# Two of the four A softmax tiles turned by VectorE and transfers instead of TensorE, in a two-layer encoder trunk

## The chip, the cores and the metric

The kernel runs on one core of one Trainium2 chip. The metric is the time of one execution in device microseconds, as the median of several runs; lower is better. TensorE (PE in the profile) multiplies and also turns 128x128 blocks, VectorE (DVE) and ScalarE (ACT) do elementwise work, GpSimd (POOL) a few small things, and SyncE (SP) issues most of the transfers (DMAs). Each engine works through a queue of its own in order.

## The reference

The model is an encoder of two layers over 256 tokens of width 1024, all in float32. Cut to what matters here:

```python
for l in range(2):
    x = x + 0.5 * swiglu(rms_norm(x, ffn1_norm[l]), ...)       # width 2816
    h = rms_norm(x, mix_norm[l])
    qa, ka, va, qb, kb, vb = jnp.split(h @ w_in[l], SPLITS, axis=-1)
    out_a = windowed_gqa_sink(qa, ka, va, sink[l], slopes_a)   # A: 8 query heads, 2 key/value heads, width 64
    out_b = differential_attention(qb, kb, vb, lam, slopes_b)  # B: 4 heads, two softmaxes each, values of width 128
    out_b = rms_norm(out_b, diff_subln[l]) * (1 - lam_init)
    x = x + jnp.concatenate([out_a, out_b], -1) @ w_out[l]
    x = x + 0.5 * swiglu(rms_norm(x, ffn2_norm[l]), ...)
return rms_norm(x, final_norm)
```

In group A a token sees the tokens within 128 of it, with a linear distance penalty, and the sum under the softmax has one more term, the head's learned sink. In group B the second softmax, times lambda, is subtracted from the first.

## The kernel before

All weights come from device memory as float32 and are split on the chip into a high part (ScalarE casts it, `act.copy`) and a low part (VectorE subtracts, `emit_split`); a product is then three matmuls (high x high, low x high, high x low). A weight tile of 1 MB is a `Step`; `specs` lists all steps in the order of use. `weights()` takes the next step and calls `ahead()`, which writes out the transfers up to ten steps ahead (six raw tiles, `N_RAW`) and the splits six half tiles ahead (seven pairs of split tiles, `N_W`). The transfers are issued on SP at line 186 and wait there until a split has freed a raw tile.

`mix(l, norm, nxt_norm)` is the attention of one layer. Its order of work:

1. Projections with the tokens on the free axis: B keys, B queries, A keys and values (`tkv`), A queries (two steps of 256 columns, `qA0`, `qA1`). `q_finish` and `k_finish` scale and split them.
2. `scores` does the products of two heads: four groups of three matmuls for each head and half, in two banks of PSUM. VectorE adds the distance penalty and takes the minimum in one instruction (`tensor_tensor_reduce`, CUSTOM_DVE in the profile); ScalarE takes the exponential with its sum. `soft_b` combines the two softmaxes of a B head on VectorE. `soft_a` handles one pair of A heads (c and c + 4): it adds the sink, takes the reciprocal, and then VectorE multiplies the four 128x256 parts by it (lines 962 to 966). Tokens are on the partitions.
3. The products with the values need the keys on the partitions. `keys_first` turns a 128x1024 tile: TensorE transposes eight 128x128 blocks into two banks, ScalarE copies one bank out and VectorE the other. It is called twice for B (`aT`) and four times for A (`pT`), so 48 transposes in each layer.
4. The B values (`vB`): two steps of four 128-row blocks (`k0` = 0 and 4), 24 matmuls each; then ScalarE scales the two halves out of PSUM. Both halves hold keys, so every B output needs both.
5. `values_a(0)` and `values_a(1)` multiply the A values with `pT`, two head pairs each, and split the results into `oT[0]` and `oT[1]`; then the B products into `osl`, `norm_b` (squares on ScalarE, sum on VectorE, power on GpSimd, product on VectorE), and `operands_b`, which turns them on TensorE into `oT[2]` and `oT[3]`.
6. The output projection: four steps of `w_out`; step k0 uses `oT[k0 // 2]`. The steps come in the order 0, 2, 4, 6, and `operands_b` stands in the middle of the second.

While `kept[0]` is true, each instruction is pinned behind the one written before it for its engine. It is set to False from the first keys to the end of part 4: there the framework's scheduler orders each engine's queue when the program is built, by readiness in its own model of time and, among ready instructions, by their place in the text. `urgent()` moves what stands in it 300 places forward in that preference. From `values_a(0)` on the written order holds.

`Blocks` is the other way of turning, in use for hidden values and norms: `take` transposes 32x32 blocks of a 128x512 half on VectorE (STREAM_TRANSPOSE), `move` issues four transfers of 128 KB from SBUF to SBUF (line 350) which carry the blocks to their partitions, and `turned` gives a view of the result. It takes two buffers of the pool `s4`, from which most tiles of the attention come as well (14 buffers).

Of the kernel before, what the change touches and what calls it, by code (L numbers as in the profile page):

```python
# [14 lines left out]
P = 128  # L15
D = 1024
# [48 lines left out]
def trunk(ctx: ExitStack, tc: tile.TileContext, x, n1, g1, u1, d1, nm, w_in, sink,  # L65
# [49 lines left out]
    def urgent():  # L115

        return tc.high_priority(300)
# [159 lines left out]
    for l in range(DEPTH):  # L277
# [52 lines left out]

# [534 lines left out]
    def ffn_close(parts, nxt, flips):  # L865
# [22 lines left out]
        res.squares(0)  # L888
        nxt.late = res.late

    def mix(l, norm, nxt_norm):
        kbs = {}
        den_b = tmp("den_b", 1, (P, HB, 4))
# [58 lines left out]
        def soft_a(c, q):  # L952
            ns = nsnk[:, l, c].rearrange("p t s -> p (t s)")
            den = den_a[:, c]
            e, negm = scores(q, kbs["a"], distA, [slopeA[c], slopeA[c + 4]], [ns[:, n:n + 1] for n in range(4)], den)
            es = tmp("es", 4, (P, 4))
            dve.tensor_tensor(es, negm, snk[:, l, c].rearrange("p t s -> p (t s)"), op=ALU.add)
            act.activation(es, es, AF.Exp)
            r = tmp("ra", 4, (P, 4))
            dve.tensor_tensor(r, den, es, op=ALU.add)  # L960
            dve.reciprocal(r, r)
            for t in range(2):
                for a in range(2):
# [8 lines left out]
        k_finish(rmul(s1), 2, [("b", 2), ("b", 3)])  # L972
        q0 = q_finish(ngroup(norm, weights()), [qscB[:, 0:1], qscB[:, 1:2]])
        q1 = q_finish(ngroup(norm, weights()), [qscB[:, 2:3], qscB[:, 3:4]])
        a_b = [soft_b(0, q0[0]), soft_b(1, q0[1])]


# [7 lines left out]
        for kc in range(2):  # L985
            pe.transpose(vsl[:, kc, 0:P], tkv[:, 1, kc * P:(kc + 1) * P], ident)
        act.copy(vA, vsl[:, :, 0:P])
        qA1 = q_finish(ngroup(norm, weights()), [qscA[:, 2:3], qscA[:, 3:4]])
        p_a = [soft_a(0, qA0[0]), soft_a(1, qA0[1])]

        def keys_first(pick):

            out_ = blk(F32)
            for kc in range(2):
                tsl = bank()
                for i in range(4):
                    pe.transpose(tsl[:, i * P:(i + 1) * P], pick(kc, i), ident)
                (act.copy if kc == 0 else dve.tensor_copy)(out_[:, kc], tsl)
            return out_

        def keys_first_b(hp):
            return keys_first(lambda kc, i: a_b[2 * hp + i // 2][:, i % 2, kc * P:(kc + 1) * P])

        def keys_first_a(c):
            return keys_first(lambda kc, i: p_a[c][:, i % 2, (i // 2) * 256 + kc * P:(i // 2) * 256 + (kc + 1) * P])

        aT = [keys_first_b(0)]
        vB = tp.tile([P, 2, 512], F32, tag="v", bufs=1, name=nm_("v"))
        vsl = [bank() for _ in range(2)]
        for k0 in (0, 4):  # L1010
            w = weights()
            for k in range(4):
                kk = k0 + k
                hi, lo = w.part(k)
                xv = norm.xs[kk // 2][:, kk % 2]
                for t in range(2):
                    xh, xl = xv[:, t * P:(t + 1) * P], xv[:, S + t * P:S + (t + 1) * P]
                    pe.matmul(vsl[t], lhsT=xh, rhs=hi, start=kk == 0, stop=False)
                    pe.matmul(vsl[t], lhsT=xl, rhs=hi, start=False, stop=False)
                    pe.matmul(vsl[t], lhsT=xh, rhs=lo, start=False, stop=kk == KC - 1)  # L1020
# [48 lines left out]
        def values_a(cp):  # L1069

            o = [bank() for _ in range(2)]
            for i in range(2):
                for kc in range(2):
                    for a in range(2):
                        j, f0 = (i + a) % 2, slice(a * 64, a * 64 + 64)
                        pe.matmul(o[j][f0, 0:S], lhsT=vA[:, kc, f0], rhs=pT[2 * cp + j][:, kc, a * 256:a * 256 + 256],
                                  start=kc == 0, stop=kc == 1)
# [13 lines left out]
        on = norm_b()  # L1091
        accs = [[bank(), bank()] for _ in range(2)]
        res = Residual(nxt_norm, accs)
# [13 lines left out]
        w = weights()  # L1107
        out_part(w, 6, 0, BY_TOKENS)
        for c in range(2):
# [115 lines left out]
```

## Time and profile before

| | |
|---|---|
| median of 3 runs | 909.76 us (909.72 to 910.09) |
| the profiled execution, its own time | 909.62 us |
| its span in the profile | 907.8 us |
| TensorE busy | 898.3 us (99%) |
| VectorE busy | 730.1 us (80%) |
| ScalarE busy | 559.7 us (62%) |
| transfers | 209.25 MB, mean 231 GB/s |

The span is what the profiler records from the first instruction to the last; 1.8 us of the execution's time lie outside of it. A row of the timeline gives the start in us, the time to the end of the last of the instructions merged in it, the engine, the line, the operation, what is written and read, the shape and the count; in brackets stands how long the engine was idle before and what released it. Almost all instructions bear line 80, a helper, so they are told apart by tiles: `s` is a buffer of the pool `s4`, `w` a split weight tile, `v` the B values, `ps` a bank of PSUM. The end of a matmul is modelled, so the pace on TensorE is taken from the starts.

### The profile page before, as it was taken

The page shows a single profiled execution, that of the slowest core. Times are in us where ns is not written, and L with a number is a line of the kernel's source. Part 1 is how long each engine was busy: PE and PEld are TensorE (multiplying, and loading weights), DVE is VectorE, ACT ScalarE, POOL GpSimd, SP SyncE. Part 2 cuts the span into 40 slices and gives each one's busy share as a digit, 9 for nine tenths or more (in the row PEclk, how much of TensorE's full clock was granted, in tenths as well). Part 3 has the DMA queues.
Part 4 walks back from the last instruction along what each step waited for, and adds up shares of the span by engine and source line. Part 5 has one row for each costly group of instructions (what it writes and reads, how often), then busy time and mean ns, then how long its engine had stood idle before and what let it go on. Part 6 is the DMA issues. An engine that isn't in the chain of part 4 may idle for free.

```text
span 907.8 us, 12665 instructions
## 1 busy us (share of the span) xinstructions
PE 898.3 (99%) x4546; PEld 756.2 (83%) x4546; DVE 730.1 (80%) x1106; ACT 559.7 (62%) x913; POOL 52.4 (6%) x72
## 2 busy tenths in 40 slices
PE   9999999999999999999999999999999999999997
PEld 7888888899888888888888888888997888888886
DVE  6689998879965789988768988887798667988883
ACT  7766665567744776665565755665676465755661
POOL 0401000000000001000000000000000000000001
PEclk9999999999999999999999999999999999999999
DMA  9989999856424879999759799997643459799921
GB/s 343 320 250 321 328 246 320 223 154 190 136 81 151 249 199 318 328 247 311 234 159 288 187 343 291 298 278 210 185 142 95 139 133 271 192 339 313 296 69 46
DMA packets 131262, 209.25 MB, mean 231 GB/s; under 512 B 5502, under 2 KB 51648, under 8 KB 131200
## 3 DMA queue, kind: packets, MB, share of 16 engines
q1 hardware_dynamic: 115808, 181.17, 60.0%
q0 software_dynamic: 12928, 25.46, 16.1%
q10 hardware_dynamic: 2464, 1.84, 0.8%
q8 instruction: 35, 0.57, 0.3%
q14 instruction: 27, 0.22, 0.1%
HBM read 192.71 MB, written 1.05 MB: 213 GB/s over the span
## 4 chain that ended last, share of the span: by engine, by line
PE 88%; DVE 5%; ACT 3%; DMA 2%; issue 2%; SPq 0%; POOLq 0%; POOL 0%; DVEq 0%; ACTq 0%
PE ps L80 88%; DVE w L80 2%; DVE s L80 2%; DMA raw<-in_ffn_w_gate_dram 1%; ACT s L80 1%; ACT w L80 1%; DMA raw<-in_ffn_w_up_dram 1%; DVE tmp L80 0%; ACT junk L80 0%; ACT tmp L80 0%; DVE ra L80 0%; ACT L80 0%; SPq L189 0%; DVE xk L80 0%; POOLq L1220 0%
## 5 line engine op out<-in xcount | busy, mean ns | idle before, releaser
L80 PE MATMUL ps<-w,s 128*128 128x512 f32 (+1 forms) x2994 | 683.2, 389 | 0.4 <-DVE s L80 0.4
L80 PEld LDWEIGHTS ps<-w,s 128*128 128x128 f32 x2994 | 558.4, 188 | 115.5 <-DVE s L80 0.7
L80 DVE TENSOR_TENSOR w<-raw,w 128x1024 fp32r<-128x1024 f32 (+1 forms) x416 | 435.1, 1087 | 97.1 <-ACT w L80 90.6
L80 ACT CAST w<-raw 128x1024 fp32r<-128x1024 f32 (+1 forms) x416 | 375.7, 942 | 172.6 <-PE ps L80 126.5
L80 PE MATMUL ps<-s,w 128*128 128x256 f32 x672 | 84.0, 285 | 0.0
L80 PEld LDWEIGHTS ps<-s,w 128*128 128x128 f32 x672 | 81.7, 191 | 1.1
L80 PE MATMUL ps<-w,q 128*128 128x512 f32 x288 | 69.4, 390 | 0.0
L80 PEld LDWEIGHTS ps<-w,q 128*128 128x128 f32 x288 | 54.0, 188 | 11.6 <-issue 0.4
L80 DVE STREAM_TRANSPOSE s<-s 128x512 f32<-128x512 f32 (+1 forms) x48 | 46.1, 999 | 0.0
L80 POOL DMA_DIRECT2D raw<-in_ffn_w_up_dram x16 | 21.0, 1314 | 400.8 <-DVE ms L80 150.1
L80 ACT CAST s<-s 128x256 fp32r<-128x256 f32 x88 | 29.3, 402 | 17.2 <-DMA s<-s 17.2
L80 ACT ACTIVATE s<-s,negm 128x256 f32<-128x256 f32 x64 | 31.9, 500 | 8.7 <-DVE negm L80 8.7
L80 DVE TENSOR_TENSOR s<-s,s 128x256 fp32r<-128x256 f32 x88 | 31.6, 421 | 5.5 <-ACT s L80 5.5
L80 ACT ACTIVATE tmp<-ps,r 128x512 f32<-128x512 f32 (+1 forms) x40 | 24.9, 644 | 13.3 <-PE ps L80 12.7
L80 ACT CAST q<-tmp 128x512 fp32r<-128x512 f32 x20 | 12.3, 616 | 31.3 <-DVE tmp L80 31.3
L80 ACT ACTIVATE junk<-xk 128x512 f32<-128x512 f32 x24 | 15.1, 631 | 19.0 <-issue 18.5
L80 PE MATMUL ps<-w,v 128*128 128x512 f32 x96 | 23.4, 391 | 0.2 <-DVE w L80 0.2
L80 ACT ACTIVATE s<-s,gcol 128x256 fp32r<-128x256 f32 (+1 forms) x40 | 17.0, 502 | 8.4 <-DMA s<-s 8.4
L80 ACT ACTIVATE tmp<-tmp,r 128x512 f32<-128x512 f32 x8 | 5.8, 725 | 26.2 <-DVE tmp L80 26.2
L80 PEld LDWEIGHTS ps<-w,v 128*128 128x128 f32 x96 | 17.9, 188 | 4.3 <-DVE w L80 0.6
L80 DVE TENSOR_TENSOR q<-tmp,q 128x512 fp32r<-128x512 f32 x20 | 14.1, 703 | 8.3 <-ACT q L80 8.3
L80 DVE SCALAR_TENSOR_TENSOR s<-ps,hr,tmp 128x512 f32<-128x512 f32 (+1 forms) x32 | 20.4, 678 | 0.0
(117 smaller groups left out, 430.7 us busy)
## 6 DMA issues: line engine op xcount, KB each, us to landing
raw<-in_ffn_w_down_dram SPq DMA_DIRECT2D x44, 1024.0 KB, 8.5
raw<-in_ffn_w_gate_dram SPq DMA_DIRECT2D x39, 1024.0 KB, 5.9
raw<-in_ffn_w_up_dram SPq DMA_DIRECT2D x39, 1024.0 KB, 7.2
raw<-in_ffn_w_up_dram POOLq DMA_DIRECT2D x16, 1024.0 KB, 10.3
raw<-in_w_in_dram SPq DMA_DIRECT2D x14, 1024.0 KB, 5.8
s<-s SPq DMA_DIRECT2D x98, 128.0 KB, 4.6
raw<-in_ffn_w_gate_dram POOLq DMA_DIRECT2D x8, 1024.0 KB, 9.8
raw<-in_ffn_w_gate_dram SPq DMA_DIRECT2D x8, 512.0 KB, 5.6
```

What stands on the lines that cost most here:

```text
L80: ins = issue(*a, **k)
```

## The change

Two of the four A softmax tiles (c = 0 and 1) go through `Blocks` instead of `keys_first`; the last multiplication of `soft_a` goes from VectorE to ScalarE for all four; and the order around them changes. `keys_first_b(0)` moves in front of the last A query projection, the second step of the B values does one half of the tokens after the other (`BY_VALUES`), `keys_first_b(1)` moves behind the B values and is `urgent`, as are the splits in `values_a`. `values_a(0)` stands between the two halves of the B products, the other two A tiles are turned on TensorE behind them, `values_a(1)` moves behind `operands_b`, and the `w_out` steps come in the order 0, 4, 2, 6 in `specs` and in use.

```diff
-        for k0 in (0, 2):
+        for k0 in (0, 4, 2, 6):
...
-            specs.append(Step(2, D, o_moves))
-        for k0 in (4, 6):
-            specs.append(plain(wo, 0, D, k0, 2))
+            specs.append(Step(2, D, o_moves) if k0 < 4 else plain(wo, 0, D, k0, 2))
...
+    BY_VALUES = {0: [(t, k) for k in range(4) for t in range(2)], 4: [(t, k) for t in range(2) for k in range(4)]}
...
-                    dve.tensor_scalar_mul(w_, w_, r[:, 2 * t + a:2 * t + a + 1])
+                    act.mul(w_, w_, r[:, 2 * t + a:2 * t + a + 1])
...
+        def keys_turned(c):
+
+            turn = Blocks(by_block=False)
+            for t in range(2):
+                turn.take(p_a[c][:, t], t)
+            turn.move()
+            return turn.turned().rearrange("p (a k) y j -> p a k y j", a=2)
...
         aT = [keys_first_b(0)]
+        qA1 = q_finish(ngroup(norm, weights()), [qscA[:, 2:3], qscA[:, 3:4]])
+        p_a = [soft_a(0, qA0[0]), soft_a(1, qA0[1])]
+
+        pT = [keys_turned(c) for c in range(2)]
...
-            for k in range(4):
+            for t, k in BY_VALUES[k0]:
...
             if k0 == 0:
                 p_a += [soft_a(2, qA1[0]), soft_a(3, qA1[1])]
-                aT.append(keys_first_b(1))
-                pT = [keys_first_a(0)]
...
-        for c in range(1, 4):
-            pT.append(keys_first_a(c))
...
-            for j in range(2):
-                split(oT[cp][:, j:j + 1], o[j][:, 0:S].unsqueeze(1))
+            with urgent():
+                for j in range(2):
+                    split(oT[cp][:, j:j + 1], o[j][:, 0:S].unsqueeze(1))
 
         kept[0] = True
-        values_a(0)
-        values_a(1)
+        with urgent():
+            aT.append(keys_first_b(1))
         osl = [bank() for _ in range(2)]
...
+            if t == 0:
+                values_a(0)
+        pT += [keys_first_a(c) for c in (2, 3)]
         on = norm_b()
...
-        for k0 in (0, 2):
+        w = weights()
+        for h in range(2):
+            out_part(w, 0, h)
+        operands_b(on)
+        values_a(1)
+        for k0 in (4, 2):
             w = weights()
             for h in range(2):
                 out_part(w, k0, h)
-                if (k0, h) == (2, 0):
-                    operands_b(on)
-        w = weights()
-        for h in range(2):
-            out_part(w, 4, h)
         w = weights()
         out_part(w, 6, 0, BY_TOKENS)
```

More of the change, by code (lines that the diff above doesn't have):

```diff
@@ L974, in mix, with keys_first, keys_first_a, keys_first_b @@
         q1 = q_finish(ngroup(norm, weights()), [qscB[:, 2:3], qscB[:, 3:4]])
+        def keys_first(pick):
+            out_ = blk(F32)
+            for kc in range(2):
+                tsl = bank()
+                for i in range(4):
+                    pe.transpose(tsl[:, i * P:(i + 1) * P], pick(kc, i), ident)
+                (act.copy if kc == 0 else dve.tensor_copy)(out_[:, kc], tsl)
+            return out_
+        def keys_first_a(c):
+            t_ = keys_first(lambda kc, i: p_a[c][:, i % 2, (i // 2) * 256 + kc * P:(i // 2) * 256 + (kc + 1) * P])
+            return t_.rearrange("p k (a y j) -> p a k y j", a=2, j=32).rearrange("p a k y j -> p a k y j")
+        def keys_first_b(hp):
+            return keys_first(lambda kc, i: a_b[2 * hp + i // 2][:, i % 2, kc * P:(kc + 1) * P])
+        def keys_turned(c):
[4 more added lines that the diff above has]
+            return turn.turned().rearrange("p (a k) y j -> p a k y j", a=2)
         a_b = [soft_b(0, q0[0]), soft_b(1, q0[1])]
@@ L987, in mix @@
         act.copy(vA, vsl[:, :, 0:P])
+        aT = [keys_first_b(0)]
         qA1 = q_finish(ngroup(norm, weights()), [qscA[:, 2:3], qscA[:, 3:4]])
         p_a = [soft_a(0, qA0[0]), soft_a(1, qA0[1])]
[L991 to L1007, printed above, removed]
+        pT = [keys_turned(c) for c in range(2)]
         vB = tp.tile([P, 2, 512], F32, tag="v", bufs=1, name=nm_("v"))
@@ L1015, in mix @@
                 xv = norm.xs[kk // 2][:, kk % 2]
[L1016 to L1020, printed above, removed]
+                xh, xl = xv[:, t * P:(t + 1) * P], xv[:, S + t * P:S + (t + 1) * P]
+                pe.matmul(vsl[t], lhsT=xh, rhs=hi, start=kk == 0, stop=False)
+                pe.matmul(vsl[t], lhsT=xl, rhs=hi, start=False, stop=False)
+                pe.matmul(vsl[t], lhsT=xh, rhs=lo, start=False, stop=kk == KC - 1)
             if k0 == 0:
                 p_a += [soft_a(2, qA1[0]), soft_a(3, qA1[1])]
-                aT.append(keys_first_b(1))
-                pT = [keys_first_a(0)]
         act.activation(vB[:, 0], vsl[0], AF.Copy, scale=norm.r[:, 0:1])
         act.activation(vB[:, 1], vsl[1], AF.Copy, scale=norm.r[:, 1:2])
-        for c in range(1, 4):
-            pT.append(keys_first_a(c))
         oT = [blk() for _ in range(4)]
@@ L1075, in values_a @@
                         j, f0 = (i + a) % 2, slice(a * 64, a * 64 + 64)
-                        pe.matmul(o[j][f0, 0:S], lhsT=vA[:, kc, f0], rhs=pT[2 * cp + j][:, kc, a * 256:a * 256 + 256],
+                        pe.matmul(o[j][f0, 0:S], lhsT=vA[:, kc, f0], rhs=pT[2 * cp + j][:, a, kc],
                                   start=kc == 0, stop=kc == 1)
-            for j in range(2):
-                split(oT[cp][:, j:j + 1], o[j][:, 0:S].unsqueeze(1))
+            with urgent():
+                for j in range(2):
+                    split(oT[cp][:, j:j + 1], o[j][:, 0:S].unsqueeze(1))
         kept[0] = True
-        values_a(0)
-        values_a(1)
+        with urgent():
+            aT.append(keys_first_b(1))
         osl = [bank() for _ in range(2)]
```

## The prediction

> **What bounds the kernel now.** I read the page's shares first, then who TensorE waited for, then TensorE's own order of work in the attention of layer 0. The page and the view of the waits:
>
> ```profile
> PE 898.3 (99%) x4546; PEld 756.2 (83%) x4546; DVE 730.1 (80%) x1106; ACT 559.7 (62%) x913; POOL 52.4 (6%) x72
> ...
> PE 88%; DVE 5%; ACT 3%; DMA 2%; issue 2%; SPq 0%; POOLq 0%; POOL 0%; DVEq 0%; ACTq 0%
> ```
>
> ```profile
> PE ps L80 <- DVE s L80: 1.6, 3, 0.6
> PE ps L80 <- DVE tmp L80: 1.4, 1, 1.4
> PE ps L80 <- DVE w L80: 0.2, 1, 0.2
> ```
>
> TensorE sets the time: it is busy almost throughout and waits 3.2 us in all. Only two things shorten this kernel, less work on TensorE and fewer of its few waits; and every new wait of TensorE is paid in full. The timeline of TensorE in the stretch that the change touches (start, us, count):
>
> ```profile
> 229.14 1.69 PE L80 MATMUL ps<-s,q 64*128 64x256 f32 x24
> 230.76 1.09 PE L80 MATMUL ps<-ident,s 128*128 128x128 f32 x8
> 231.61 5.74 PE L80 MATMUL ps<-w,s 128*128 128x512 f32 x24
> 237.28 1.69 PE L80 MATMUL ps<-s,q 64*128 64x256 f32 x24
> 238.90 1.09 PE L80 MATMUL ps<-ident,s 128*128 128x128 f32 x8
> 239.74 4.84 PE L80 MATMUL ps<-w,s 128*128 128x512 f32 x20
> 244.42 1.04 PE L80 MATMUL ps<-ident,s 128*128 128x128 f32 x8
> 245.21 1.17 PE L80 MATMUL ps<-w,s 128*128 128x512 f32 x4
> 246.22 1.03 PE L80 MATMUL ps<-ident,s 128*128 128x128 f32 x8
> 247.88 2.45 PE L80 MATMUL ps<-ident,s 128*128 128x128 f32 x16 [0.62 <-DVE s L80]
> 250.26 3.67 PE L80 MATMUL ps<-s,vA 128*64 128x256 f32 x32
> 253.86 3.84 PE L80 MATMUL ps<-v,s 128*128 128x128 f32 x32
> 257.45 8.44 PE L80 MATMUL ps<-w,s 128*128 128x512 f32 x36
> 265.74 1.03 PE L80 MATMUL ps<-ident,s 128*128 128x128 f32 x8
> ```
>
> Eight transposes take 0.85 (230.76 to 231.61), 0.84 and 0.79 us: 0.10 each. From 244.42 to 250.26, 5.84 us, stand 32 transposes of the four A tiles and four matmuls (1.01 us). At 0.10 the 32 would take 3.2; so 1.63 us of waiting lie in this stretch, some of it marked (0.62 for the multiplied weights), some inside the merged rows. Layer 1 shows the same (693.95, again 0.62), so I work out one layer and double it.
>
> ```profile
> 693.95 2.45 PE L80 MATMUL ps<-ident,s 128*128 128x128 f32 x16 [0.62 <-DVE s L80]
> ```
>
> **The change, part by part.** TensorE loses the transposes of c = 0 and 1: 16 x 0.10 = 1.6 us. The other 16 move behind work that doesn't need them, so the 1.63 us of waiting can go too: at most 3.2 us a layer. Where TensorE would then stand, with no new wait, is a sum of starts. The A queries end 0.85 later, since the first B tile is turned in front of them: 229.99. Scores 1.62, B values 5.67, scores 1.62, B values 5.69, the second B tile 0.84: the B products start at 245.43. Half of them (3.59 / 2 = 1.80) to 247.23, `values_a(0)` (3.60 / 2 = 1.80) to 249.03, the other half to 250.83, 16 transposes to 252.43; there `w_out` 0 starts. Before it starts at 257.45, but with `values_a(1)` behind it, so the break-even is 257.45 - 1.80 = 255.65.
>
> Now what must be ready at these times. ScalarE gets the 16 multiplications. Rows of it, by group on the page and from the timelines:
>
> ```profile
> L80 ACT ACTIVATE s<-s,negm 128x256 f32<-128x256 f32 x64 | 31.9, 500 | 8.7 <-DVE negm L80 8.7
> ```
>
> ```profile
> 231.76 0.51 ACT L80 ACTIVATE s<-s,negm 128x256 f32<-128x256 f32 x1 [0.93 <-DVE negm L80]
> ...
> 237.44 1.12 ACT L80 CAST w<-raw 128x512 fp32r<-128x512 f32 x2
> ...
> 237.96 2.19 DVE L80 TENSOR_SCALAR s<-s,ra 128x256 f32<-128x256 f32 x8
> ...
> 246.80 0.28 ACT L80 ACTIVATE es<-es 128x4 f32<-128x4 f32 x2
> 246.99 0.56 ACT L80 COPY s<-ps 128x512 f32<-128x512 f32 x1
> ...
> 247.46 1.25 ACT L80 ACTIVATE v<-ps,r 128x512 f32<-128x512 f32 x2
> ...
> 252.33 0.65 ACT L80 CAST s<-ps 128x256 fp32r<-128x256 f32 x2 [1.44 <-PE ps L80]
> ```
>
> ```profile
> 290.82 1.71 ACT L80 ACTIVATE s<-s,gcol 128x256 fp32r<-128x256 f32 x4 [0.64 <-DMA s<-s]
> ```
>
> VectorE did a multiplication in 2.19 / 8 = 0.27. A 128x256 part by a per-partition factor on ScalarE is the row at 290.82: 1.71 / 4 = 0.43, so 6.8 us for 16. The Trainium skill, ScalarE: Activation LUTs, section Rules for kernel authors, gives multiplications to VectorE and not to ScalarE, which speaks against this part; the rows agree, 0.43 against 0.27. By the rule, with the 16 left on VectorE, ScalarE's sum below would be 14.4 us in place of 21.2, and VectorE's 4.4 more.
>
> Is ScalarE free for it? From the first exponential of the A heads (231.76 before, 0.85 later after: 232.6) it has, until the last weights are multiplied: 16 exponentials at 0.50 = 8.0, three pairs of weight casts at 1.12 = 3.4, two rows of sinks at 0.28 = 0.6, the multiplications 6.8, the B values out of PSUM 1.25, a copy for the second B tile 0.56, the split of `values_a(0)` 0.65: 21.2 us. That ends at 253.8 if it is never idle. The eight transposes of c = 3 need the last of it, where TensorE alone would be there at 251.6. So ScalarE is the **new bound** of this stretch: `w_out` 0 starts at 253.8 + 0.8 = 254.6, not at 252.43. Against 255.65 that gains 1.05 us. If the last pair of casts falls behind the multiplications, as nothing needs it soon, it is 2.2; if ScalarE idles 1.1 us for data, nothing. I take 1.2 us a layer, the middle.
>
> VectorE loses 16 x 0.27 = 4.4 us and two copies, and gets four block transposes:
>
> ```profile
> 308.82 2.04 DVE L80 STREAM_TRANSPOSE s<-s 128x512 f32<-128x512 f32 x2
> 310.78 2.32 DVE L80 TENSOR_TENSOR w<-raw,w 128x1024 fp32r<-128x1024 f32 x2
> 310.92 2.50 SPq L350 DMA_DIRECT2D s<-s  x4
> ```
>
> ```profile
> 158.02 2.52 SPq L350 DMA_DIRECT2D s<-s  x4
> ...
> 163.01 0.71 ACT L80 CAST s<-s 128x256 fp32r<-128x256 f32 x2 [0.35 <-DMA s<-s]
> ```
>
> Two transposes take 2.04, so 4.1 us; VectorE is relieved. Four transfers take SP 2.5 us to issue, and from the first issue to the use 5.0 us pass (158.02 to 163.01, with a wait for the transfer at the end). The multiplications of c = 0, 1 began at 237.96 before. One after the other from 238.0 on ScalarE, c = 0 is done at 239.7, c = 1 at 241.4; their block transposes end at about 240.8 and 242.8. SP issues c = 0 to 243.3, then c = 1; it lands 5.0 after 243.3, at 248.3. `values_a(0)` wants it at 247.2: 1.1 us late, but the wait for ScalarE comes earlier or covers it, so I don't add it.
>
> SP carries eight more issues, 5 us, and its weight loads stand behind them:
>
> ```profile
> SPq L186 <- DVE ra L80: 16.9, 2, 8.5
> ```
>
> ```profile
> 237.67 0.37 SPq L186 DMA_DIRECT2D raw<-in_ffn_w_up_dram  x1
> 246.57 28.23 SPq L186 DMA_DIRECT2D raw<-in_ffn_w_gate_dram  x4
> ```
>
> The load at 237.67 had waited 8.5 us for its raw tile, without any wait of TensorE for weights; I cost loads that come 5 us later at nothing, and at up to 1 us a layer if the splits run late.
>
> `norm_b` must be done when `w_out` 0 ends. Before:
>
> ```profile
> 257.74 0.60 ACT L80 ACTIVATE tmp<-ps 128x512 f32<-128x512 f32 x1 [1.19 <-PE ps L80]
> ...
> 261.09 1.29 DVE L80 TENSOR_TENSOR s<-ps,rb 128x512 f32<-128x512 f32 x2 [1.75 <-POOL rb L80]
> ```
>
> From the end of the B products (257.45) to the scaled result (262.38) pass 4.93 us; after, 16 transposes and 24 matmuls (7.3 us) cover it, less the two copies in front of the squares on ScalarE (about 2 us). It holds by some tenths. Between `operands_b` and `w_out` 4 stands `values_a(1)`, 1.8 us, beside the 12 matmuls that covered it before (2.8); I cost that at 0 to 0.5. The order of the `w_out` loads moves no bytes. Matmuls that read `pT` in runs of 32 are shown nowhere; nothing below, and 1.8 us a layer above if `values_a(0)` took twice its time; as the nearest row, the plain `values_a`, is not limited by reading, I take nothing.
>
> The sum: 2 x 1.2 = 2.4 us less. The profiled execution took 909.62 with a span of 907.8; from the median of 909.76 it gives **907.4 us**. Its own range is 2 x 0 to 2 x 2.2, so 905.3 to 909.8.
>
> **The rivals.**
>
> *Full gain.* The scheduler puts casts and multiplications so that ScalarE is never waited for: 2 x 3.2 = 6.4, 903.4 us. For it: TensorE's own sum. Against: 21.2 us of ScalarE in 21.2 us. Chance 0.14.
>
> *Nothing.* What TensorE saves comes back whole as waits for ScalarE, or the saved transposes only move the wait: 909.6, within 1.8 us either way. Chance 0.12.
>
> *The B values late* (the other side). The two activations that take `vB` out of PSUM stand behind `soft_a(2)` and `soft_a(3)` in the text and are not urgent. The matmuls of `vB` end at 244.6, where ScalarE is in the second eight exponentials. If those and the eight multiplications go first, `vB` comes at about 252.6 (253.8 less copy and split), and then the B products, `values_a(0)` and the transposes still follow: 5.4 + 1.6, `w_out` 0 at 259.6, 4.0 late, 2 x 4.0 = 8.0: 917.8 us. It decides from 248.65 on (255.65 less 7.0): any `vB` later than that makes the kernel slower. For it: before, `vB` came only behind the last row of sinks (246.80, then 247.46). Against: gaps in which the sums are awaited. Chance 0.16, mostly between 911.6 and 915.
>
> *The turn late.* If the scheduler puts the eight transfers behind the load that is issued at 246.57, they are issued from 246.9, those of c = 1 from 249.4, and land at 254.4, 7.2 us after TensorE wants them; less the 3.2 gained this is 4.0 a layer, 917.8 us. Break-even is a landing at 250.4, 2.1 us later than I worked out. For it: SP's queue is in order, and that load waits there for a split. Against: its place in the text is behind them. Chance 0.10, mostly 911.6 to 914. The Trainium skill, VectorE: DVE Perf Modes, section Rules for kernel authors, gives a 128x128 transpose to TensorE where PSUM will do as the destination; by that rule the kernel loses in this way. The rows agree on the prices, 0.8 us on TensorE against 2.04 and 5.0 of latency for one tile, but not yet on who pays them.
>
> **How the numbers follow.** 0.2% is 1.8 us, about what a measurement of this kernel can tell from no change. The forecast has 0.48, of which 0.14 lies within 0.2% (the upper part of its own range). Faster: 0.34 + 0.14 = 0.48. Same: 0.14 + 0.12 = 0.26. Slower: 0.16 + 0.10 = 0.26. For 8 in 10 the range leaves out half of the full gain below (0.07) and the far half of the two late cases above (0.13): 904.0 to 913.5.
>
> **What would show it.** TensorE: 16 transposes fewer for each layer, and the starts from 229.99 to `w_out` 0 as summed, with waits named. Right: `w_out` 0 about 1.2 us ahead of its break-even, ScalarE busy without a gap from 232 to 253, TensorE's waits for `s` or `v` by ScalarE about 2 us a layer. The full gain shows no waits; the late B values show one long wait ahead of the `v` products, the late turn one ahead of `values_a(0)`, released by a transfer. I am wrong altogether if TensorE waits in the feed-forward parts, for weights: then the loads on SP, costed at nothing, decide.

## The result and the profile after

| | median (range), runs | ratio to before, 95% interval |
|---|---|---|
| before | 909.92 us (909.61 to 910.57), 14 | |
| after | 911.85 us (910.24 to 913.95), 14 | 1.0019 [1.0012, 1.0026] |

The change makes the kernel slower by 0.19%, where 907.4 us was forecast. The spread is as telling as the median: before lies within 1 us, after within 3.7 us. Five runs of after took 910.24 to 910.44 with a mean granted clock (the share of its full speed that TensorE was given) of 0.999; the other nine took 911.55 to 913.95 with a clock of 0.994 to 0.997. The profiled execution is one of the nine: 913.5 us, span 911.7, clock 0.996 (before: 909.62, 907.8, 0.999).

The page of after, the engines:

```profile
PE 899.0 (99%) x4514; PEld 755.4 (83%) x4514; DVE 727.8 (80%) x1078; ACT 570.2 (63%) x941; POOL 53.0 (6%) x72
```

TensorE has the 32 instructions less that it should have (4546 to 4514), and yet is busy for 0.7 us longer: something made its instructions slower. The view of TensorE's waits:

```profile
PE ps L80 <- DVE s L80: 2.5, 3, 1.1
PE ps L80 <- ACT v L80: 2.0, 2, 1.0
```

The view's four rows sum to 6.4 us of waits, where before had 3.2. One kind is new, for the B values `v` by ScalarE, 0.98 us in each layer. The other, for a tile `s` by VectorE, was there before with 0.62 in each layer, ahead of the transposes; it is now 1.07 and stands ahead of the B products. TensorE's timeline shows where, layer 0 first:

```profile
245.68 0.39 PE L80 MATMUL ps<-v,s 128*128 128x128 f32 x2
247.05 1.45 PE L80 MATMUL ps<-v,s 128*128 128x128 f32 x8 [0.98 <-ACT v L80]
249.57 0.94 PE L80 MATMUL ps<-v,s 128*128 128x128 f32 x6 [1.07 <-DVE s L80]
250.43 1.95 PE L80 MATMUL ps<-s,vA 128*64 128x256 f32 x16
252.31 2.05 PE L80 MATMUL ps<-v,s 128*128 128x128 f32 x16
254.20 1.91 PE L80 MATMUL ps<-ident,s 128*128 128x128 f32 x16
255.87 5.70 PE L80 MATMUL ps<-w,s 128*128 128x512 f32 x24
```

The first half of the B products starts at 245.68 and ends at 250.43: 4.75 us for work of 1.80. These 2.95 us are nearly all of the 3.2 us a layer that the shorter and reordered work could save. `w_out` 0 starts at 255.87. The break-even was 255.65, and after is already 0.3 late ahead of the stretch (the row of 24 score products: 237.61 against 237.28 before), so layer 0 gains 0.1 us in the stretch. By the exit it has lost 0.34 again: from `w_out` 0 to the end of the output projection before needs 22.92 us (257.45 to 280.37), after 25.06 (255.87 to 280.93), of which 1.80 is the moved `values_a(1)`.

Layer 1 has the same two waits, and then it is different:

```profile
695.88 1.65 PE L80 MATMUL ps<-v,s 128*128 128x128 f32 x6 [1.07 <-DVE s L80]
697.46 3.68 PE L80 MATMUL ps<-s,vA 128*64 128x256 f32 x16
701.08 2.62 PE L80 MATMUL ps<-v,s 128*128 128x128 f32 x16
703.54 1.91 PE L80 MATMUL ps<-ident,s 128*128 128x128 f32 x16
```

By the starts, the six B products take 1.58 us where layer 0 needs 0.86, the sixteen `values_a` 3.62 for 1.88, the next sixteen 2.46 for 1.89: 3.0 us more for the same instructions. The windows of after say why (stretch, length, then busy time and count of PE, PEld, DVE, ACT and POOL, then the granted clock, the DMA share and GB/s):

```profile
694.00:696.00 2.00, 0.90 (x6) 0.52 (x4) 1.90 (x5) 2.00 (x8) 0.00 (x0) 0.87 0.83 183
696.00:698.00 2.00, 2.00 (x10) 1.58 (x12) 0.47 (x4) 1.59 (x7) 0.00 (x0) 0.50 0.81 202
698.00:700.00 2.00, 2.00 (x12) 1.13 (x10) 0.00 (x0) 2.00 (x6) 0.00 (x0) 0.50 0.83 323
700.00:702.00 2.00, 2.00 (x10) 1.16 (x7) 0.40 (x2) 0.79 (x3) 0.00 (x0) 0.50 0.00 0
702.00:704.00 2.00, 2.00 (x19) 2.00 (x19) 0.35 (x2) 0.00 (x0) 0.00 (x0) 0.93 0.00 0
```

TensorE's granted clock is halved from about 695.5 to 702.3: 0.87 over 2 us is 0.52 us at half, 0.93 is 0.28, so 6.8 us in all. The profiled execution is then accounted for: at the exit of layer 0 after is 0.56 late (0.33 from ahead of the stretch, -0.11 in it, 0.34 behind it), at that of layer 1 3.84 (730.28 against 726.44): 3.0 for the clock, the 0.56 brought along from layer 0, and 0.25 of its own. The first 0.33 us arise in the first feed-forward part, whose code is unchanged: at 60.73 us TensorE has waited 0.49 for a split weight tile, where before waited 0.16. Why that wait differs stays open.

Why was TensorE kept waiting? The timelines of VectorE, ScalarE and SP's queue in after, layer 0:

```profile
240.36 4.07 DVE L80 STREAM_TRANSPOSE s<-s 128x512 f32<-128x512 f32 x4
244.34 0.46 DVE L80 CUSTOM_DVE_ANT_0 s<-ps,distA,nsnk 128x256 f32<-128x256 f32 x1
...
248.82 0.69 DVE L80 COPY s<-ps 128x512 f32<-128x512 f32 x1
```

```profile
239.42 3.31 ACT L80 ACTIVATE s<-s,ra 128x256 f32<-128x256 f32 x8
242.63 0.67 ACT L80 ACTIVATE v<-ps,r 128x512 f32<-128x512 f32 x1
...
244.84 0.51 ACT L80 ACTIVATE s<-s,negm 128x256 f32<-128x256 f32 x1 [0.28 <-DVE negm L80]
...
246.33 0.67 ACT L80 ACTIVATE v<-ps,r 128x512 f32<-128x512 f32 x1
...
250.53 3.30 ACT L80 ACTIVATE s<-s,ra 128x256 f32<-128x256 f32 x8 [0.41 <-DVE ra L80]
```

```profile
242.53 5.39 SPq L348 DMA_DIRECT2D s<-s  x8
```

Three things reach TensorE late, one closely behind the other. TensorE is done with the second half of `vB` when the transposes of `aT[1]` begin (244.80); ScalarE takes it out of PSUM at 246.33, behind three exponentials, until 247.0. TensorE is done with `aT[1]` at 245.68; the half of the copy that VectorE does starts at 248.82, because the four block transposes (4.07 us) stand ahead of the eight minima in its queue, and these, with a weight split behind them, ahead of the copy. In before the minima start at 241.27, by VectorE's timeline there:

```profile
241.27 0.48 DVE L80 CUSTOM_DVE_ANT_0 s<-ps,distA,nsnk 128x256 f32<-128x256 f32 x1
```

And the eight transfers of the turn are issued one after another, 242.53 to 247.9; the view of line 348 gives 2.7 us from issue to landing, so the last of them (247.3) lands at 250.0, 0.4 us ahead of its use.

### The profile page after: what moved, and what is told of

It is laid out like the page before. It is cut to its first block, busy times and chain, and to the rows that moved or that the text cites. A ratio compares the mean times of both kernels' runs of the same rounds, so it can differ in the third digit from the quotient of the medians.

```text
span 911.7 us, 12629 instructions
## 1 busy us (share of the span) xinstructions
PE 899.0 (99%) x4514; PEld 755.4 (83%) x4514; DVE 727.8 (80%) x1078; ACT 570.2 (63%) x941; POOL 53.0 (6%) x72
## 4 chain that ended last, share of the span: by engine, by line
PE 92%; DVE 4%; ACT 2%; issue 1%; POOLq 0%; POOL 0%; DVEq 0%; ACTq 0%
PE ps L80 92%; DVE s L80 2%; DVE w L80 1%; ACT s L80 1%; ACT w L80 1%; DVE tmp L80 0%; ACT tmp L80 0%; ACT L80 0%; DVE ra L80 0%; DVE xk L80 0%; POOLq L1229 0%; POOL rf L80 0%; DVEq L1229 0%; DVE negm L80 0%; ACTq L80 0%
## 5 line engine op out<-in xcount | busy, mean ns | idle before, releaser
L80 DVE STREAM_TRANSPOSE s<-s 128x512 f32<-128x512 f32 (+1 forms) x56 | 54.3, 1013 | 0.1
```

The costliest lines, as they stand in the source:

```text
L80: ins = issue(*a, **k)
```

## The experiments

**The theories.** V: VectorE's queue is the cause; the block transposes ahead of the minima push back the copy of `aT[1]` and the exponentials, and with them the rest. S, the rival and the reasoning of the prediction: ScalarE has more work than time, and any work taken off it helps. Beside both stands the claim that the halved clock comes from TensorE's standing still, and isn't a cause of its own. Diffs are against the kernel after, unless said otherwise; "before" on the same chips had medians of 909.79 to 909.88.

| run | what | median (range), runs | ratio to before | granted clock |
|---|---|---|---|---|
| e1_fill | idle matmuls in the two waits | 910.74 (910.54 to 911.46), 11 | 1.0010 [1.0001, 1.0019] | 0.998 to 1.000 |
| e2_no_turn | all A tiles on TensorE | 937.24 (936.97 to 938.12), 4 | 1.0303 [1.0288, 1.0317] | 0.984 to 0.986 |
| e3_no_mul | multiplications on VectorE | 919.17 (916.69 to 919.43), 4 | 1.0096 [1.0082, 1.0110] | 0.991 to 0.995 |
| e4_order_only | e2 and e3 together | 927.16 (925.41 to 927.84), 4 | 1.0187 [1.0173, 1.0201] | 0.989 to 0.991 |
| e5_no_turn_late | e2, transposes behind the B values | 919.37 (917.15 to 920.24), 4 | 1.0101 [1.0087, 1.0115] | 0.994 to 0.996 |
| e6_order_late | e5 and multiplications on VectorE | 911.74 (911.53 to 912.42), 10 | 1.0021 [1.0012, 1.0030] | 0.998 to 0.999 |
| e7_early_urgent | second B tile early, `vB` urgent | 912.40 (911.94 to 913.36), 6 | 1.0031 [1.0018, 1.0043] | 0.994 to 0.996 |
| e8_one_turn | e7 with only c = 0 turned by VectorE | 913.78 (912.11 to 915.33), 5 | 1.0042 [1.0029, 1.0055] | 0.995 to 0.998 |
| e9_vb_first | second B tile early, `vB` pinned first | 911.79 (910.61 to 912.90), 11 | 1.0020 [1.0011, 1.0029] | 0.997 to 0.999 |
| e10_late_values | e9, `values_a(0)` later, c = 3 on VectorE | 907.69 (906.96 to 907.87), 9 | 0.9972 [0.9962, 0.9981] | 0.998 to 0.999 |
| e11_two_queues | e9, c = 3 on VectorE, two DMA queues | 910.72 (910.54 to 912.14), 11 | 1.0011 [1.0002, 1.0020] | 0.998 to 0.999 |
| e12_before_mul | before, multiplications on ScalarE | 915.51 (915.05 to 915.58), 5 | 1.0058 [1.0046, 1.0071] | 0.996 to 0.997 |

**e1_fill.** Idle matmuls with nothing to wait for are put into the two waits; the computation is unchanged.

```diff
                 for kc in range(2):
                     c0 = (h % 2) * 256 + t * P
+                    for _ in range({(0, 0, 1): 5, (0, 2, 1): 7}.get((t, h, kc), 0)):
+                        pe.matmul(osl[1][:, 0:P], lhsT=ident, rhs=ident, start=True, stop=True)
```

> The changed kernel with idle matmuls of the identity put ahead of the two places where TensorE waits in the B products: five in front of the first product with the second half of vB, seven in front of the first product with the second bank of aT[1] (each two instructions, 0.22 us in all, so 1.1 and 1.5 us). They go to a bank that is started afresh afterwards. Theory (the clock of TensorE drops because it stands still twice within 5 us): granted clock 0.999 in every run, time 910.3 within 0.3 in all runs, as in those runs of the changed kernel that had 0.999; the waits themselves stay, so it isn't faster than that. Rival (the drops come from something else in the change, such as matmuls that read pT in runs of 32, or the transfers beside them): runs between 910.3 and 914 with clocks down to 0.994 stay, median about 911.9.

TensorE's timeline of e1_fill:

```profile
246.43 1.28 PE L80 MATMUL ps<-ident 128*128 128x128 f32 x10
...
248.87 1.73 PE L80 MATMUL ps<-ident 128*128 128x128 f32 x14
250.43 0.83 PE L80 MATMUL ps<-v,s 128*128 128x128 f32 x6
```

The fillers are a little too long (the six products start at 250.43, 0.3 us later against their entry than in after), and still the median is 1.1 us lower and no run has a clock below 0.998. That settles the clock of after: it falls because TensorE stands still there, and with it goes all of the spread above 911.5 us. What is left, 910.74, is slightly slower than before: the waits alone take the gain.

**e2_no_turn and e4_order_only.** The turn goes back to TensorE, written in its place ahead of the B values; e4 takes the multiplications back as well.

```diff
-        pT = [keys_turned(c) for c in range(2)]
+        pT = [keys_first_a(c) for c in range(2)]
```

> The changed kernel with c = 0 and 1 turned on TensorE again (keys_first_a in place of keys_turned), all else as changed. TensorE gets 16 transposes a layer back, 1.6 us. Theory V (the four block transposes, 4.07 us on VectorE in front of the second minima, make everything behind them late): the second minima begin at about 241.3 in place of 244.34, the two waits of 2.95 us a layer shrink to under 1 us, and the time is 909 to 909.5, a little under 910.3, without clock drops. Rival S (ScalarE's 21 us of work bound the stretch, as forecast): the waits stay at 2 to 3 us and the transposes come on top, 912.5 to 913.5.

> Only the new order: no block transposes, multiplications on VectorE; 32 A transposes a layer on TensorE as before. Theory V: nothing stands ahead of the second minima but 2.19 us of multiplications; waits under 1 us a layer in place of the 1.63 of before: 907.5 to 909, clock 0.999. Rival S agrees on the sign, as ScalarE has what it had before, 908. If instead it is slower than before, the order itself (B values ahead of values_a, later vB against aT) is at fault, 911 to 912.

Neither tells what it was meant to tell. TensorE's timeline of e2:

```profile
238.53 2.77 PE L80 MATMUL ps<-ident,s 128*128 128x128 f32 x10 [6.39 <-ACT s L80]
```

In e4 the same row has waited 6.18 us, for VectorE. The scheduler put the first transposes ahead of the B values in TensorE's queue, where their tile was not yet multiplied. Over 6 us a layer of that wait come from my place in the text, not from the part undone. e5 and e6 do it again with the place put right.

**e3_no_mul.**

```diff
-                    act.mul(w_, w_, r[:, 2 * t + a:2 * t + a + 1])
+                    dve.tensor_scalar_mul(w_, w_, r[:, 2 * t + a:2 * t + a + 1])
```

> The changed kernel with the multiplications of soft_a on VectorE again, all else as changed. Theory V: VectorE gets 2.19 us for each two tiles back on the chain that ends the second wait, ahead of the block transposes, less the time that it stood waiting for ScalarE there (0.7 us): the waits grow by 0.5 to 1.5 us a layer, time 911.5 to 913 before any clock drop. Rival S: ScalarE's sum falls from 21.2 to 14.4 us, the waits go, 904 to 907.

This decides against S. ScalarE lost 6.6 us a layer of work (16 at 3.31 / 8 = 0.41), and the kernel became 7.3 us slower. e3's TensorE, and its VectorE (from 239 us on, so the first row shows six of the eight multiplications):

```profile
250.88 1.65 PE L80 MATMUL ps<-v,s 128*128 128x128 f32 x6 [4.39 <-DVE s L80]
```

```profile
238.90 1.66 DVE L80 TENSOR_SCALAR s<-s,ra 128x256 f32<-128x256 f32 x6
...
241.69 4.13 DVE L80 STREAM_TRANSPOSE s<-s 128x512 f32<-128x512 f32 x4
...
246.90 0.48 DVE L80 CUSTOM_DVE_ANT_0 s<-ps,distA,nsnk 128x256 f32<-128x256 f32 x1
...
250.14 0.69 DVE L80 COPY s<-ps 128x512 f32<-128x512 f32 x1
```

The wait for `v` is gone, the wait for VectorE's copy has grown from 1.07 to 4.39 us in each layer: the minima start 2.6 us later still, and the copy is behind all of them. The direction is V's; the time is above V's range, and the clock adds to it: e3's windows show 0.50 from 252 to 254 and 0.56 from 701 to 703, behind this wait in both layers.

**e5_no_turn_late and e6_order_late.** Turn on TensorE again, now written behind the B values; e5 keeps the multiplications on ScalarE, e6 gives them back to VectorE and so is the change of order alone.

```diff
-        pT = [keys_turned(c) for c in range(2)]
...
         act.activation(vB[:, 1], vsl[1], AF.Copy, scale=norm.r[:, 1:2])
+        pT = [keys_first_a(c) for c in range(2)]
```

> The changed kernel with c = 0 and 1 turned on TensorE, this time written behind the B values, so that TensorE doesn't stand in front of them for weights that aren't there. Theory V (VectorE's four block transposes, ahead of the second minima, set the waits): the second minima begin 3 us earlier than in the changed kernel, the waits fall from 2.95 to 0.3 to 1 us a layer, TensorE has 1.6 us more: 907 to 909, clock 0.999. Rival S (ScalarE's multiplications set them): the waits stay at 2 us or more, 911 to 914.

> The new order alone with the A tiles of c = 0 and 1 turned on TensorE behind the B values and the multiplications on VectorE. Against the kernel before this leaves only the order. Theory V: the multiplications (2.19 us for two tiles) stand ahead of the second minima as before; waits 0.5 to 1.2 us a layer against 1.63 before: 908 to 909.5, clock 0.999. If the order as such costs time, 911 or more.

e5 goes against V as the whole cause: without a block transpose on VectorE no wait of the B products for VectorE is left, and yet the kernel is 7.5 us slower than after. Its TensorE, and its ScalarE:

```profile
249.30 0.94 PE L80 MATMUL ps<-v,s 128*128 128x128 f32 x6 [1.28 <-ACT v L80]
252.32 1.66 PE L80 MATMUL ps<-v,s 128*128 128x128 f32 x8 [2.09 <-ACT s L80]
```

```profile
248.56 0.68 ACT L80 ACTIVATE v<-ps,r 128x512 f32<-128x512 f32 x1
...
250.09 1.71 ACT L80 ACTIVATE s<-s,ra 128x256 f32<-128x256 f32 x4
251.69 0.58 ACT L80 COPY s<-ps 128x512 f32<-128x512 f32 x1
```

Now ScalarE's queue is in the wrong order: `vB` behind exponentials and casts, the copy that TensorE wants behind four multiplications that nobody needs yet. e6, the order alone, has the same two waits in small, and is slower than before by 1.9 us, where 908 to 909.5 us was expected under V:

```profile
248.55 0.94 PE L80 MATMUL ps<-v,s 128*128 128x128 f32 x6 [0.73 <-ACT v L80]
249.98 1.16 PE L80 MATMUL ps<-v,s 128*128 128x128 f32 x8 [0.49 <-ACT s L80]
```

Together with e3 and after this is a square: order alone 911.74; order and multiplications (e5) 919.37; order and turn (e3) 919.17; all three (after) 911.85. Each of the two other parts alone costs some 7.5 us, and together they take each other's cost back: the turn fills VectorE and the multiplications empty it; the multiplications fill ScalarE and the turn takes copies off it. (In e5 and e6 the place of the transposes was my choice, so the corners are not exact.)

**e7_early_urgent and e8_one_turn.** If VectorE's copy is late, the second B tile can be turned before the B values; and `urgent` should bring `vB` forward. e8 leaves only c = 0 with VectorE, and gives c = 1 back to TensorE.

```diff
+        aT.append(keys_first_b(1))
         pT = [keys_turned(c) for c in range(2)]
...
-        act.activation(vB[:, 0], vsl[0], AF.Copy, scale=norm.r[:, 0:1])
-        act.activation(vB[:, 1], vsl[1], AF.Copy, scale=norm.r[:, 1:2])
+        with urgent():
+            act.activation(vB[:, 0], vsl[0], AF.Copy, scale=norm.r[:, 0:1])
+            act.activation(vB[:, 1], vsl[1], AF.Copy, scale=norm.r[:, 1:2])
```

> The changed kernel with the second B tile written ahead of the B values (so its copy doesn't stand behind the second minima on VectorE) and with the two activations that take vB out of PSUM made urgent. The two waits that the changed kernel shows are taken away at their place. Theory (three late things stand one behind the other, and the last transfer of the turned weights lands at 250.0): TensorE comes to values_a(0) at about 247.3 and waits there for the transfers until 250: one wait of 2.5 us in place of two of together 2.95, 909.4 to 910.3, with clock drops on top in some runs. Rival S (ScalarE): the waits go to the multiplications of c = 2, 3, same time. If the transfers are early enough after all, 905.

> As e7, but only c = 0 goes through VectorE and transfers; c = 1 is turned on TensorE ahead of the B products. VectorE has 2.04 us less ahead of the second minima, SP issues four transfers in place of eight, which land by about 247.3 in place of 250.0; TensorE has 0.8 us more a layer than the changed kernel. Theory V: waits under 0.8 us a layer, 906 to 908, clock 0.999, the best so far. Rival S: ScalarE has the same 21 us, 909 to 911.

Both missed. In e7 the wait for VectorE is gone, and the wait for `vB` has taken its place; TensorE in both layers of e7:

```profile
247.86 3.36 PE L80 MATMUL ps<-v,s 128*128 128x128 f32 x14 [1.98 <-ACT v L80]
...
695.06 1.83 PE L80 MATMUL ps<-v,s 128*128 128x128 f32 x14 [1.98 <-ACT v L80]
...
698.28 1.91 PE L80 MATMUL ps<-s,vA 128*64 128x256 f32 x14 [0.82 <-DMA s<-s]
```

`urgent` had not moved `vB`: by ScalarE's timeline of e7 it is taken out at 247.14, behind four exponentials. In layer 1 the next late thing shows itself, the landing of the turn. In e8 the scheduler put the second half of `vB` behind all eight exponentials (wait 2.67 us), so it says nothing on the number of turns. The one standstill of e7 in layer 0 also halved the clock, for one stretch of 3.4 us (window view of e7, clock in the third column from the end):

```profile
247.80:251.20 3.40, 3.34 (x16) 3.12 (x16) 1.71 (x8) 2.99 (x14) 0.00 (x0) 0.50 0.79 162
```

**e9_vb_first.** So `vB` is pinned: the exponentials of c = 2 and 3 are written behind its two activations and kept there.

```diff
+        aT.append(keys_first_b(1))
         pT = [keys_turned(c) for c in range(2)]
...
             if k0 == 0:
-                p_a += [soft_a(2, qA1[0]), soft_a(3, qA1[1])]
+                sc = [products(qA1[i], kbs["a"]) for i in range(2)]
...
         act.activation(vB[:, 1], vsl[1], AF.Copy, scale=norm.r[:, 1:2])
+        st = [soft_a(2 + i, qA1[i], sc[i]) for i in range(2)]
+        p_a += [soft_a2(2 + i, *st[i]) for i in range(2)]
...
+                    if pin:
+                        tc.keep_in_program_order(x_)
```

> The changed kernel with the second B tile turned ahead of the B values, and with ScalarE's exponentials for c = 2, 3 pinned behind the two activations that take vB out of PSUM (their products on TensorE stay where they are). Unlike e7 this really moves vB ahead on ScalarE. Theory (the turned weights are late next): the wait ahead of the second half of vB goes (under 0.4 us left), TensorE comes to values_a(0) at about 247.5 and waits for the transfers until 250.0, one wait of 2.5 us; w_out 0 starts at about 255.4 in layer 0 (255.87 in the changed kernel), 909.4 without and 911 to 913 with clock drops. Rival: if vB alone had been the cause, w_out 0 at 253.5 and 905 to 906.

TensorE of e9, layer 0:

```profile
246.56 1.83 PE L80 MATMUL ps<-v,s 128*128 128x128 f32 x14 [0.56 <-ACT v L80]
...
250.35 1.91 PE L80 MATMUL ps<-s,vA 128*64 128x256 f32 x14 [1.39 <-DMA s<-s]
```

`vB` now costs 0.56 us, the copy nothing, and the time is the same: the wait has gone to the third in line, the turn, 1.39 us here and 2.21 in layer 1. Two of the 16 matmuls of `values_a(0)` run at 248.32, but the other 14 not before 250.35; in after all 16 started at 250.43. The place of the wait is as expected, the time is not: the profiled execution kept its clock (0.999) and took 911.37 us, where 909.4 was expected without clock drops.

**e10_late_values and e11_two_queues.** Two ways around that. e10 puts `values_a(0)` behind both halves of the B products, so that 1.8 us of work that is ready covers the landing. e11 leaves it and issues half of the transfers on GpSimd's queue, so that they go out in parallel. Both give the multiplications of c = 3 back to VectorE.

```diff
-                    act.mul(w_, w_, r[:, 2 * t + a:2 * t + a + 1])
+                    (dve.tensor_scalar_mul if c == 3 else act.mul)(w_, w_, r[:, 2 * t + a:2 * t + a + 1])
...  e10 alone
-            if t == 0:
+            if t == 1:
                 values_a(0)
...  e11 alone
-            turn.move()
+            turn.move((sp, pool))
```

> As e9, with values_a(0) behind both halves of the B products, so that 1.8 us of work stand in front of the turned weights, and with the multiplications of c = 3 on VectorE, which is idle by then, so that both tiles are multiplied at about 252. Theory (three late things, one behind the other, each a place in a queue): B products from 245.5 to 249.2, wait for the transfers 0.8 us, then nothing; w_out 0 at about 254.0, 1.9 us a layer earlier than in the changed kernel: 906 to 907, clock 0.999, faster than the kernel before. Rival (ScalarE's sum, as forecast): ends at 253.8 with 1.65 us less to do, so 252.2; it would not show here. If the time is above 909, something else is late that I have not seen.

> As e10, but values_a(0) stays between the halves of the B products, and the block transfers are issued from two queues, SP and GpSimd, two each for a tile. If the landing at 250.0 is due to the eight issues in one queue (0.67 us each), the transfers land by about 248 to 248.5: wait under 1 us, w_out 0 at about 253.7, 906. If GpSimd's issues take their 1.3 us and land later than SP's, nothing is won: 908 to 911, with one long wait ahead of values_a(0) released by a transfer.

TensorE of e10:

```profile
246.42 3.62 PE L80 MATMUL ps<-v,s 128*128 128x128 f32 x30 [0.56 <-ACT v L80]
249.97 2.23 PE L80 MATMUL ps<-s,vA 128*64 128x256 f32 x16
252.12 2.17 PE L80 MATMUL ps<-ident,s 128*128 128x128 f32 x16
254.05 5.74 PE L80 MATMUL ps<-w,s 128*128 128x512 f32 x24
```

Behind the first wait for `vB` the B products run through. No wait for the turn is marked here (in layer 1 one of 0.56 us), `w_out` 0 starts at 254.05, 1.6 us ahead of the break-even, the clock stays at 0.998 or more in all nine runs. e10 beats both kernels: 907.69 us, 2.2 below before, though 0.7 above the range expected for it. e11 doesn't; its TensorE still waits for the transfers:

```profile
251.36 1.91 PE L80 MATMUL ps<-s,vA 128*64 128x256 f32 x14 [1.33 <-DMA s<-s]
```

The four transfers on GpSimd's queue land 3.7 to 4.8 us after their issue in layer 0. That is not a matter of GpSimd's queue alone: the four left on SP's now take 2.8 to 5.2 us there (median 4.4), where the median of all eight on SP's was 2.7 in after and in e9. In layer 1 it is even a transfer of SP's that TensorE waits for, 1.2 us. So with two queues the transfers of both land later, which gives back what the parallel issue saves; why they do was not tested. The two kernels differ in these two edits only, so none of the 3.0 us between them belongs to the multiplications of c = 3; the wait that the place of `values_a(0)` removes, 1.3 us in each layer of e11 (0.56 of it left in layer 1 of e10), accounts for 2.0 of them; the rest is not traced. What those multiplications are worth against e9 was not run alone, and neither was the later `values_a(0)` without the two repairs of e9.

**e12_before_mul.** Before, with nothing but the 16 multiplications of each layer on ScalarE.

```diff
-                    dve.tensor_scalar_mul(w_, w_, r[:, 2 * t + a:2 * t + a + 1])
+                    act.mul(w_, w_, r[:, 2 * t + a:2 * t + a + 1])
```

> The kernel before with one part of the change alone: the multiplications of soft_a on ScalarE. There the first two A tiles are turned amid the B values and the last two right behind them, so each multiplication is on the way to TensorE. Theory: 0.41 us a piece in place of 0.27, so the last eight end 1.1 us later and the waits grow by 1 to 2 us a layer, and as two tiles are awaited apart, clock drops may come: 912 to 916. If the multiplications don't matter for the end, 909.8.

5.6 us slower. TensorE waits for the multiplications of c = 2 and 3 themselves, and takes its transposes piece by piece as they are done; on ScalarE they stand behind exponentials, a cast, a copy and half of `vB`. Its TensorE, and its ScalarE:

```profile
248.89 0.44 PE L80 MATMUL ps<-ident,s 128*128 128x128 f32 x2 [1.63 <-ACT s L80]
```

```profile
248.34 3.30 ACT L80 ACTIVATE s<-s,ra 128x256 f32<-128x256 f32 x8
```

Before, VectorE's eight began at 247.47 and took 2.19 us. So 0.9 us a layer of the delay is the place in the queue and 1.1 the slower instruction; on top, the granted clock falls to 0.50 behind the wait in layer 0 (252 to 254).

The rule of the Trainium skill that the prediction named (ScalarE: Activation LUTs, Rules for kernel authors: multiplications to VectorE) thus holds where it is applied alone, and e3 shows its reverse: with the turn on VectorE, following it costs 7.3 us. In e12 the price of the instruction, 0.41 against 0.27 us, is 1.1 of the 2.0 us by which the multiplications end later; in e3 the cheaper instruction loses, because the copy that TensorE wants stands behind it in VectorE's queue.

## Why the prediction was wrong, point by point

- **TensorE's own sum** was right. The B products were to start at 245.43 and start at 245.68 with the entry 0.3 late; a 128x128 transpose on TensorE costs 0.10; at most 3.2 us a layer were to be had.
- **The step that failed**: "ScalarE is the new bound of this stretch: `w_out` 0 starts at 253.8 + 0.8 = 254.6". The sum of ScalarE's work was taken for the date of its last piece, and that date for the bound. ScalarE had gaps (0.28 us for the minima, 0.41 for the reciprocals in the rows of after), and yet its multiplications ended at 253.8 as summed, in part by luck: the split of `values_a(0)`, 0.65 us of the sum, came behind them (253.74), and gaps took its place. But `w_out` 0 came at 255.87 and not at 254.6: TensorE was held up earlier, at the B products, by the place of two single instructions in the queues, ScalarE's half of `vB` (0.98 us marked) and VectorE's copy (1.07), with 2.95 us of standing in all. e3 took 6.6 us off ScalarE and made it worse. TensorE came to its last 16 transposes only at 254.20, behind the date that was taken for the bound, so after does not show what that date would have cost alone.
- **"VectorE is relieved"** was the other half of that step. It has less work, but 4.07 us of it stand in one piece ahead of the minima, 3 us later than before, and the copy of `aT[1]` comes behind them. The prediction costed the copy (0.56 on ScalarE) and never asked when VectorE gets to its half.
- **The turn**: landing at 248.3 was forecast, 250.0 came. The multiplications began at 239.42 and not at 238.0, behind a pair of casts, and eight issues took 5.4 us rather than 5.0. "The wait for ScalarE comes earlier or covers it, so I don't add it" was true of after, and is the reason why e9 gained nothing (and a part of it in layer 1 of e7, 0.82 us): the landing was the next bound, 0.4 us ahead of its use.
- **The rivals** were each right about a place. `vB` does stand behind exponentials (247.0, break-even 248.65), the turn is late (250.0, break-even 250.4); neither reaches its break-even alone. I weighed them one at a time, as cases that exclude each other. They are three dates that are all late, with the copy's; the last of them counts, and TensorE's 2.95 us of standing is what is left of the 3.2.
- **The clock** was in no term. Where it doesn't fall, in the five runs of 910.24 to 910.44, the result is that of the rival "nothing" (909.6, within 1.8 either way); the median of all is 911.85, inside the range for 8 in 10 (904.0 to 913.5) but on the other side of no change than forecast.
- **Costed at nothing and held**: SP's later weight loads (TensorE's only wait for `w`, 0.49 us against 0.16, lies in the first feed-forward part, ahead of them), `norm_b` (`operands_b` follows `w_out` 0 without a marked wait, 261.41), and the reads of `pT` in runs of 32. That last term was put at nothing because the plain `values_a` "is not limited by reading", for which no row was shown; the runs bear the nothing out, for in after the 16 matmuls of `values_a(0)` take 1.88 us and those of `values_a(1)`, which read in the plain way, as well (262.40 to 264.28). `values_a(1)` in its new place is inside the 0.34 us lost behind `w_out` 0, as allowed (0 to 0.5).

## What to carry to other kernels

When work moves between two engines of which neither is the bound, don't add up their work: write down, for each thing that the bounding engine will ask for, the queue it comes through and what stands ahead of it there. Look for the second and third late thing before paying for the removal of the first; here three of them lay within 3.0 us (247.0, 249.5, 250.0). Bringing two of them forward (e9) gained nothing; with the use of the third (`values_a(0)`) moved back as well, the gain came (e10). Two parts of a change can each cost 7 us alone and nothing together, so one part undone is no price of that part.

## What the runs showed of the hardware

Standing still can cost TensorE twice. All pauses here are taken by the starts (the time from one start to the next, less the 0.11 to 0.12 us that each matmul between takes). The pauses of after are short, 1.15 and 1.62 us with 0.90 us of work between (245.68 to 249.57), and yet in layer 1 of the profiled execution they set off 6.8 us at half the clock, which costs 3.0 us of time. In layer 0 of the same execution the same pauses set off nothing.

Over the kernels, pauses of 0.90 and 0.76 (e6, ten runs), of up to 0.98 (e10, nine) and of up to 1.72 (e11, 11) never brought the clock below 0.998. Those of after did in nine runs of 14, and those of e7 (2.14, and in layer 1 1.23 more) in all six. Filled with idle matmuls (e1), none of 11 runs fell. The length of the longest pause doesn't settle it: e9 has one of 2.59 in layer 1 and fell below 0.998 in only two runs of 11, and not in the profiled one.

The Trainium skill, TensorE: Matmul & The Clock Gate, section What's actually happening, describes a gate that looks at the activity in free-running windows of about 3.4 us and grants half the clock after an idle one. The 0.50 and the 3.4 us of e7's stretch agree with it, and free-running windows would make the effect a matter of chance from run to run, as it is in after; but no window was idle here: in after TensorE worked for 1.1 of the 3.9 us. What share of a window decides was not measured.
